# The second SwiGLU product as seven block products in three slabs of K

## The chip, the cores and the metric

The kernel runs on one core of a Trainium2 chip. The metric is the device time of one execution in microseconds (us): 2076.77 us is the median of three runs of the kernel before, which lie between 2076.21 and 2076.93 us. The engines are called PE (matrix products), DVE, ACT and POOL (elementwise work), and SP (which issues the transfers).

## The reference

One layer of a hybrid encoder on 1024 tokens of width 1024, in float32: a normalisation, two mixers in parallel with a residual, then a normalisation, a SwiGLU and a residual, and a last normalisation. The change touches only the SwiGLU and what follows it:

```
def swiglu(xn, w_ffn_in, w_ffn_out):
    gate, up = _split(xn @ w_ffn_in, (D_FF, D_FF))
    return (jax.nn.silu(gate) * up) @ w_ffn_out

h = h + swiglu(rms_norm(h, norm2_g[l]), w_ffn_in[l], w_ffn_out[l])
return rms_norm(h, norm_f)
```

D_FF is 2816, which is 22 tiles of 128. The first product is 1024 tokens by 1024 by 5632, the second 1024 tokens by 2816 by 1024.

## The kernel before

Every large product is done on operands that are split in two: `split` (L79 to L81) casts a float32 source to its high part on ACT and subtracts that from the source on DVE, which gives the low part. A product of two split operands takes three matmuls: high by high, high by low and low by high. The DVE half of a split reads two tensors in SBUF.

The first SwiGLU product goes through 22 units of 128 gate columns and 128 up columns. A unit's weight is four blocks, and so are the tokens, and the four products of a unit come from seven block products instead of eight. POOL makes four sums of weight blocks for each unit (`unit_sums`, L798 to L801), `weight` splits a block or a sum, `product` (L810) issues the matmuls, and `after` adds the banks up. The list `seq` gives the order of the seven products over the units; weights are prepared four products ahead. Each unit's result `act` is written to `act_dram`.

The second product is a plain one. It goes through six pieces of K of 2, 4, 4, 4, 4 and 4 tiles. For each piece and each of the eight groups of 128 tokens, `mm_tok` (L143) runs three matmuls for each tile of K and each half of the columns, and DVE adds the bank to `hres` (L1063; ACT copies it for the first piece, L1061). Its operands are reloaded from `act_dram` and from `w_ffn_out` through `w_raw` (`load_next`, L92) and split by `split_next` once for each group of tokens. The residual `hl` is added to `hres` by POOL (L1055) in the piece that begins at tile 6. In the last piece each group of tokens ends with its own normalisation and two transfers to the output (L1078, L1080); the last group does its second half of columns in two cuts, which go to banks of their own:

```
cuts = (0, 512, 768, 1024) if last and c == NC - 1 else (0, 512, 1024)
...
    po = bank("mm" if c % 2 else "aux")[:, :b - a]
```

All engines run their instructions in the order in which the built program has them. A scheduler puts the instructions of each engine in order when the program is built, so the order is not quite that of the source. Tiles of one tag share a number of buffers (`slot0` and `slot1` have eight each of 8 KB for a partition), and an instruction that writes a new tile waits for the last reader of the buffer that it takes.

Of the kernel before, what the change touches and what calls it, by code (L numbers as in the profile page):

```python
# [32 lines left out]
def hybrid_block_kernel(  # L33
# [426 lines left out]
    with phase("ssd") as pp:  # L460
# [533 lines left out]
    for nk in (2, 4, 4, 4, 4, 4):
        wf = [[], []]
        pieces.append((f0, nk, wf))
        for n in range(2):
            for q in range(nk // 2):
                add_act(f0 + n * (nk // 2) + q)
                add_wf(n, q, f0, wf)  # L1000
        f0 += nk
# [37 lines left out]
    with phase("ffn_out", "right") as pp:  # L1039
        g_bc = pp.tile([P, D], F32, name="g_bc7")  # L1040
        nc.sync.dma_start(out=g_bc, in_=norm_f.unsqueeze(0).broadcast_to([P, D]))

        for f0, nk, wf in pieces:
            last = f0 + nk == NFT
            for c in range(NC):
                if plan or loaded:
                    split_next()
                cuts = (0, 512, 768, 1024) if last and c == NC - 1 else (0, 512, 1024)
                if last:
                    o = pp.tile([P, D], F32, name="o7", tag="o7", bufs=2)  # L1050
                    ss = pp.tile([P, 4], F32, name="ss7", tag="ss7", bufs=3)
                if f0 == 6:
                    hl = pp.tile([P, D], F32, name="hl", tag="hl", bufs=2)
                    nc.sync.dma_start(out=hl, in_=h_dram[c * P:(c + 1) * P, :])
                    nc.gpsimd.tensor_tensor(out=hres[c], in0=hres[c], in1=hl, op=ALU.add)  # L1055
                for i, (a, b) in enumerate(zip(cuts, cuts[1:])):
                    ns, ws = slice(a, b), slice(a % 512, a % 512 + b - a)
                    po = bank("mm" if c % 2 else "aux")[:, :b - a]
                    mm_tok(po, lambda p, k: acts[f0 + k][:, p, c * P:(c + 1) * P], lambda p, k: wf[a // 512][p][:, k, ws], nk)
                    if not f0:  # L1060
                        nc.scalar.copy(out=hres[c][:, ns], in_=po)  # L1061
                        continue
                    nc.vector.tensor_tensor(out=hres[c][:, ns], in0=po, in1=hres[c][:, ns], op=ALU.add)  # L1063
                    if last:
                        nc.scalar.activation(out=o[:, ns], in_=hres[c][:, ns], func=AF.Square, accum_out=ss[:, i:i + 1])
                        if i == 0 and c == NC - 1:
                            nc.gpsimd.tensor_tensor(out=hres[c][:, ns], in0=hres[c][:, ns], in1=g_bc[:, ns], op=ALU.mult)
                if last:
                    nc.vector.tensor_tensor(out=ss[:, 0:1], in0=ss[:, 0:1], in1=ss[:, 1:2], op=ALU.add)
                    if c == NC - 1:  # L1070
                        nc.vector.tensor_tensor(out=ss[:, 0:1], in0=ss[:, 0:1], in1=ss[:, 2:3], op=ALU.add)
                    r = rsqrt_act(pp, ss[:, 0:1], 1.0 / D)
                    for n in range(2):
                        ns = half(n)
                        if n == 0 and c == NC - 1:
                            nc.scalar.activation(out=o[:, ns], in_=hres[c][:, ns], func=AF.Copy, scale=r[:, 0:1])
                        else:
                            nc.vector.scalar_tensor_tensor(out=o[:, ns], in0=hres[c][:, ns], scalar=r[:, 0:1],  # L1078
                                                           in1=g_bc[:, ns], op0=ALU.mult, op1=ALU.mult)
                        nc.sync.dma_start(out=out[c * P:(c + 1) * P, ns], in_=o[:, ns])  # L1080


# [30 lines left out]
```

## Time and profile before

| what | value |
|---|---|
| median of three runs | 2076.77 us |
| profiled execution | 2076.53 us |
| its span, first to last instruction | 2074.8 us |
| granted TensorE clock, mean | 0.993 |
| PE, DVE, ACT, POOL busy | 97%, 59%, 40%, 25% |
| second product in the trace | about 1818.8 to 2066.9 us |

The span is the time between the first and the last instruction of the profiled execution; 1.7 us of its time lie around the span. A PE that is shown busy is pipelined: the rate is read from the distance between groups of matmuls. In a timeline each row has the start, the time taken, the engine, the line, and what it writes and reads; a row can stand for several instructions (x24).

### The profile page before, as it was taken

What the parts mean: (1) busy time and instruction counts of PE and PEld (TensorE: products, weight loads), DVE (VectorE), ACT (ScalarE), POOL (GpSimd) and SP (SyncE); (2) the same over time, 40 slices, a digit from 0 to 9 for tenths busy, and PEclk for the clock granted to TensorE, in tenths of its full rate; (3) what the DMA queues carried; (4) which work ended last, traced back from release to release, by engine and by line L of the source; (5) the groups of instructions that cost most, each with busy time, mean ns of one, the idle gap of its engine ahead of it and who ended that gap; (6) DMA issues with size and microseconds to landing.
All of it is one profiled execution on the core that took longest, in us unless ns stands there. A gap on an engine that the chain in (4) does not pass through costs nothing.

```text
span 2074.8 us, 23723 instructions
## 1 busy us (share of the span) xinstructions
PE 2014.5 (97%) x9212; PEld 1652.6 (80%) x9212; DVE 1215.4 (59%) x1906; ACT 837.7 (40%) x1172; POOL 520.6 (25%) x364
## 2 busy tenths in 40 slices
PE   5999999999999999899999999998999999999998
PEld 4778888878788788688888888886888888888887
DVE  7677676887877877624432123567555555546445
ACT  5877653554544544531131113344323233342112
POOL 3101004525526436300101100036433433303000
PEclk9999999999999999999999999999999999999999
DMA  4221241231322322323232112521232232256212
GB/s 134 62 68 58 61 127 51 88 100 57 92 82 67 110 73 62 101 86 93 63 115 61 51 41 82 191 93 62 72 102 72 71 102 81 76 187 194 82 61 81
DMA packets 178804, 182.27 MB, mean 88 GB/s; under 512 B 9404, under 2 KB 145028, under 8 KB 178692
## 3 DMA queue, kind: packets, MB, share of 16 engines
q1 hardware_dynamic: 178692, 180.76, 28.0%
q8 instruction: 72, 1.18, 0.2%
q14 instruction: 40, 0.33, 0.1%
HBM read 148.10 MB, written 32.64 MB: 87 GB/s over the span
## 4 chain that ended last, share of the span: by engine, by line
PE 78%; DVE 11%; DMA 3%; POOL 2%; issue 2%; ACT 2%; SPq 0%; POOLq 0%; DVEq 0%; ACTq 0%
PE mm L132 35%; PE mm L810 20%; PE mm L143 13%; PE aux L143 6%; DMA ed<-acs_dram 2%; DVE rs_t L155 1%; DVE ed L541 1%; DMA w_raw<-in_w_in_dram 1%; PE aux L421 1%; PE aux L587 1%; DVE rs_r L156 1%; DVE xd L612 1%; DVE wz L81 1%; DVE rs_t L154 1%; PE turn L512 1%
## 5 line engine op out<-in xcount | busy, mean ns | idle before, releaser
L810 PE MATMUL mm<-slot,wc 128*128 128x512 f32 x1848 | 426.9, 392 | 6.3 <-DVE slot L914 5.1
L810 PEld LDWEIGHTS mm<-slot,wc 128*128 128x128 f32 x1848 | 346.9, 188 | 84.7 <-DVE slot L914 6.7
L132 PE MATMUL mm<-xn_hi,w_hi 128*128 128x512 f32 x896 | 354.1, 395 | 1.6 <-DVE xs_a L312 1.1
L132 PE MATMUL mm<-xn_hi,w_lo 128*128 128x512 f32 x896 | 353.3, 395 | 0.0
L132 PE MATMUL mm<-xn_lo,w_hi 128*128 128x512 f32 x896 | 352.2, 393 | 1.1 <-DVE xn_lo L202 1.1
L143 PE MATMUL mm<-slot,slot 128*128 128x512 f32 (+1 forms) x924 | 213.6, 387 | 0.0
L132 PEld LDWEIGHTS mm<-xn_lo,w_hi 128*128 128x128 f32 x896 | 169.2, 189 | 38.7 <-DVE xn_lo L202 1.4
L132 PEld LDWEIGHTS mm<-xn_hi,w_hi 128*128 128x128 f32 x896 | 169.2, 189 | 38.3 <-DVE xs_a L312 1.9
L143 PEld LDWEIGHTS mm<-slot,slot 128*128 128x128 f32 x924 | 171.5, 188 | 34.8
L132 PEld LDWEIGHTS mm<-xn_hi,w_lo 128*128 128x128 f32 x896 | 169.1, 189 | 37.1
L81 DVE TENSOR_TENSOR w_lo<-w_raw,w_hi 128x1024 fp32r<-128x1024 f32 x80 | 108.1, 1351 | 138.4 <-ACT w_hi L80 138.3
L143 PE MATMUL mm<-wz,xn_hi 128*128 128x512 f32 x512 | 164.0, 398 | 0.0
L80 ACT CAST w_hi<-w_raw 128x1024 fp32r<-128x1024 f32 x80 | 83.5, 1043 | 172.9 <-PE mm L132 152.1
L143 PE MATMUL aux<-slot,slot 128*128 128x512 f32 x528 | 124.4, 389 | 0.0
L143 PEld LDWEIGHTS aux<-slot,slot 128*128 128x128 f32 x528 | 99.1, 188 | 20.6
L143 PEld LDWEIGHTS mm<-wz,xn_hi 128*128 128x128 f32 x512 | 96.0, 190 | 18.9
L143 PE MATMUL mm<-wz,xn_lo 128*128 128x512 f32 x256 | 101.8, 398 | 0.0
L848 POOL TENSOR_TENSOR u_u<-u_u,e 128x512 f32<-128x512 f32 x22 | 28.8, 1310 | 248.2 <-DVE u_u L842 238.4
L81 DVE TENSOR_TENSOR wc<-s,wc 128x512 fp32r<-128x512 f32 x88 | 76.4, 908 | 23.0 <-ACT wc L80 23.0
L132 PE MATMUL mm<-v_even,w_hi 128*128 128x512 f32 x256 | 84.7, 405 | 2.2 <-ACT v_even L201 2.2
L132 PE MATMUL mm<-v_odd,w_hi 128*128 128x512 f32 x256 | 81.9, 398 | 0.0
L80 ACT CAST slot<-w_raw 128x1024 fp32r<-128x1024 f32 x34 | 35.5, 1051 | 110.2 <-PE mm L143 50.0
(273 smaller groups left out, 3298.0 us busy)
## 6 DMA issues: line engine op xcount, KB each, us to landing
w_raw<-in_w_in_dram SPq DMA_DIRECT2D x72, 512.0 KB, 3.9
ed<-acs_dram SPq DMA_DIRECT2D x32, 512.0 KB, 3.6
w_raw<-in_w_branch_dram SPq DMA_DIRECT2D x24, 512.0 KB, 3.5
w_raw<-in_w_ffn_in_dram SPq DMA_DIRECT2D x22, 512.0 KB, 4.1
raw_pair<-in_w_ffn_in_dram SPq DMA_DIRECT2D x22, 512.0 KB, 4.3
act_dram<-act SPq DMA_DIRECT2D x22, 512.0 KB, 2.6
act_raw<-act_dram SPq DMA_DIRECT2D x22, 512.0 KB, 3.5
w_raw<-in_w_ffn_out_dram SPq DMA_DIRECT2D x22, 512.0 KB, 4.7
```

The source lines that it names most:

```text
L80: nc.scalar.copy(out=hi, in_=src)
L81: nc.vector.tensor_tensor(out=lo, in0=src, in1=f32(hi), op=ALU.subtract)
L132: nc.tensor.matmul(ps[:m, :], ww[:, k, :], xx(p, k, h), start=(k == 0 and i == 0), stop=(k == nk - 1 and i == 2))
L143: nc.tensor.matmul(ps, xx(p, k), ww(q, k), start=(k == 0 and i == 0), stop=(k == nk - 1 and i == 2))
L154: nc.vector.tensor_tensor(out=t, in0=r, in1=r, op=ALU.mult)
L155: nc.vector.scalar_tensor_tensor(out=t, in0=t, scalar=-0.5, in1=v, op0=ALU.mult, op1=ALU.mult)
L156: nc.vector.scalar_tensor_tensor(out=r, in0=t, scalar=1.5, in1=r, op0=ALU.add, op1=ALU.mult)
L421: nc.tensor.matmul(pg, w[:, j, :], uu[:, hs], start=(q == 0), stop=(q == 2))
L512: nc.tensor.transpose(out=pt[:, i * P:(i + 1) * P], in_=raw[:, o:o + P], identity=ident)
L541: nc.vector.tensor_tensor(out=ed, in0=ed, in1=bcast(acs_t[:, c, hs], P), op=ALU.subtract)
L810: nc.tensor.matmul(ps, w[:, p, k, :], x[q][:, k, :], start=(start and k == 0 and i == 0), stop=(k == 3 and i == 2), skip_group_check=True)
L848: nc.gpsimd.tensor_tensor(out=d["u3"], in0=d["u3"], in1=d["e5"], op=ALU.add)
```

## The change

The second product is written as seven block products instead of eight. Tokens are cut in two halves, columns in two halves, and K in three slabs of 6, 8 and 8 tiles, each cut in two halves of 3, 4 and 4 tiles. In each slab seven products run in the order 1, 2, 6, 7, 5, 4, 3; each has 3 or 4 steps (one for each tile of a half of K), and a step is 12 matmuls of 512 columns, three for each of four groups of tokens. Four loads (roles 1 to 4) bring a quarter of the tokens' operand and a quarter of the weight each, for all steps of a slab; the raw tiles and the split ones share the buffers of `slot0` and `slot1`. For each step's tile of K, eight sums or differences of 128x512 are made of the raw tiles, seven of them on POOL (`slab_sums`, `slab_sums_late`) and one on DVE (L1027). The four banks of a product are added to `hres` or to a sum `vsum` when the product ends.

The two last units of the first product now run side by side in `seq`, and the loads and the first splits of slab 0 are issued during them. The final normalisation is done for tokens 512 to 1023 after product 4 of the last slab and for the others after product 3. The last group of tokens still has its second half in two cuts, both now in one bank.

```diff
+    SLABS = ((0, 3), (6, 4), (14, 4))
...
+    def slab_load(s, role):
+        f0, kk = SLABS[s]
+        i = 1 if role in (1, 3) else 0
+        ti, ka = {1: (0, 0), 2: (0, 1), 3: (1, 0), 4: (1, 1)}[role]
+        kb, dj = {1: (0, 0), 2: (1, 0), 3: (0, 1), 4: (1, 1)}[role]
+        for k0 in range(0, kk, 2):
+            n = min(2, kk - k0)
+            t = pair_tile(i, f"p{role}")
+            fa, fb = f0 + ka * kk + k0, f0 + kb * kk + k0
+            nc.sync.dma_start(out=t[:, :n, 0, :], in_=act_dram[fa * P:(fa + n) * P, half(ti)].rearrange("(k p) m -> p k m", p=P))
+            nc.sync.dma_start(out=t[:, :n, 1, :], in_=w_cols(w_ffn_out, dj * 512, 512, fb * P, n))
...
+    def slab_sums(s, k):
+        p1, p2, p3, p4 = (rawp[s, i, k] for i in range(1, 5))
+        x = xs12[s, k]
+        nc.gpsimd.tensor_tensor(out=x[:, 0], in0=p3[:, 0], in1=p4[:, 0], op=ALU.add)
+        nc.gpsimd.tensor_tensor(out=x[:, 1], in0=p3[:, 1], in1=p1[:, 1], op=ALU.subtract)
+        nc.gpsimd.tensor_tensor(out=p3[:, 0], in0=p1[:, 0], in1=p3[:, 0], op=ALU.subtract)
+        nc.gpsimd.tensor_tensor(out=p1[:, 0], in0=x[:, 0], in1=p1[:, 0], op=ALU.subtract)
+        nc.vector.tensor_tensor(out=p1[:, 1], in0=p4[:, 1], in1=x[:, 1], op=ALU.subtract)
+
+    def slab_sums_late(s, k):
+        p1, p2, p3, p4 = (rawp[s, i, k] for i in range(1, 5))
+        nc.gpsimd.tensor_tensor(out=p3[:, 1], in0=p4[:, 1], in1=p3[:, 1], op=ALU.subtract)
+        nc.gpsimd.tensor_tensor(out=p2[:, 0], in0=p2[:, 0], in1=p1[:, 0], op=ALU.subtract)
+        nc.gpsimd.tensor_tensor(out=p2[:, 1], in0=p2[:, 1], in1=p1[:, 1], op=ALU.subtract)
...
+    y, z = NFT - 2, NFT - 1
+    seq += [(y, 2), (z, 1), (y, 6), (z, 2), (z, 6), (y, 5), (z, 5), (y, 7), (z, 7), (y, 3), (z, 3), (y, 4), (z, 4)]
...
+    EVAC = {1: "11", 2: "11", 6: "v", 7: "22", 5: "22", 4: "21", 3: "12"}
+    ORDER = (1, 2, 6, 7, 5, 4, 3)
...
+    def slab_prepare(i):
...
+        if (s, r, k) not in steps_hl:
+            slab_step(s, r, k)
+        if r == 1 and k == 0:
+            slab_sums_first(s)
+        if r == 2:
+            slab_sums(s, k)
+        if r == 6:
+            slab_sums_late(s, k)
+        if s < 2 and last_k:
+            if r == 6:
+                slab_load(s + 1, 1)
+            elif r == 7:
+                slab_load(s + 1, 3)
+            elif r == 3:
+                slab_load(s + 1, 2)
+                slab_load(s + 1, 4)
...
+    def last_product(ps, kk):
+        for c in range(4):
+            cuts = (slice(0, 512),) if c < 3 else (slice(0, 256), slice(256, 512))
+            for i, cols in enumerate(cuts):
+                for k in range(kk):
+                    step_mm(ps[c], steps_hl[2, 3, k], c, False, k == kk - 1, cols)
+                evac_block(2, 3, c, ps[c], cols)
...
+    SLEAD = 4
```

Three places show what the built program made of it.

POOL from the end of the first product on, before. The names are the units' sums (`u_u`), then the residual sums into `hr`:

```order
L848 TENSOR_TENSOR u_u_13084<-u_u_13084,e_13108 128x512
L848 TENSOR_TENSOR u_u_13214<-u_u_13214,e_13236 128x512
L1055 TENSOR_TENSOR hr_13322<-hr_13322,hl 128x1024
L1055 TENSOR_TENSOR hr_13323<-hr_13323,hl 128x1024
L1055 TENSOR_TENSOR hr_13324<-hr_13324,hl 128x1024
```

The same place now, slab 0. `p_13108` is role 1, `p_13148` role 2, `p_13252` role 3, `p_13172` role 4, each with steps 0 and 1; the names in 13111, 13151, 13255 and 13175 hold step 2 of the same roles. The waits are shown:

```order
L1023 TENSOR_TENSOR x_sums<-p_13252,p_13172 128x512 [waits DMAHW7_49,DMAHW5_49,PE_49]
L1024 TENSOR_TENSOR x_sums<-p_13252,p_13108 128x512 [waits DMAHW4_49,DMAHW0_49]
...
L1024 TENSOR_TENSOR x_sums<-p_13255,p_13111 128x512 [waits DMAHW6_49,DMAHW2_49]
L1025 TENSOR_TENSOR p_13252<-p_13108,p_13252 128x512 [waits Pool_49]
L1031 TENSOR_TENSOR p_13252<-p_13172,p_13252 128x512 [waits DMAHW6_49,Pool_49]
L1033 TENSOR_TENSOR p_13148<-p_13148,p_13108 128x512 [waits DVE_49,Activation_49]
...
L1033 TENSOR_TENSOR p_13151<-p_13151,p_13111 128x512 [waits DMAHW4_49,DVE_49,Activation_49]
L1026 TENSOR_TENSOR p_13108<-x_sums,p_13108 128x512 [waits Pool_49] x2
L1026 TENSOR_TENSOR p_13111<-x_sums,p_13111 128x512 [waits Pool_49]
```

POOL had the eight residual sums there and nothing else. It now has 21 sums, and L1026, whose result product 6 multiplies, stands as the 16th to 18th of them, behind six of L1023 and L1024 and nine of L1025, L1031 and L1033. The first of the 21 waits for a count of PE, which PE reaches as it comes to the slab's first matmul; in slab 1 the count is reached 24 matmuls ahead of the slab, in slab 2 again at its first matmul.

POOL in slab 1, now; `p_13455` and `p_13683` are roles 1 and 2 of steps 2 and 3:

```order
L1032 TENSOR_TENSOR p_13680<-p_13680,p_13452 128x512
L1026 TENSOR_TENSOR p_13455<-x_sums,p_13455 128x512
L1163 TENSOR_TENSOR hr_13331<-hr_13331,hl 128x1024
L1163 TENSOR_TENSOR hr_13332<-hr_13332,hl 128x1024
L1026 TENSOR_TENSOR p_13455<-x_sums,p_13455 128x512
```

The second L1026 here is the one that step 3 of product 6 multiplies. From the slab's first L1023 to it there are 30 instructions, four of them the wide residual sums of L1163; two of those stand right before it. In slab 2 the same count is 29, all of 128x512, with four of L1153 among them.

PE at the program's end, before, where the last group of tokens does its second half in two cuts (the buffers' numbers are kept out; each cut starts a bank of its own):

```order
L143 MATMUL mm<-slot_14352,slot_14518 128x512
L143 MATMUL mm<-slot_14484,slot_14319 128x256
L143 MATMUL mm<-slot_14485,slot_14319 128x256
...
L143 MATMUL mm<-slot_14485,slot_14518 128x256
L143 MATMUL mm<-slot_14484,slot_14518 128x256
```

and now:

```order
L1124 MATMUL aux<-hl_step 128x512 x9
L1124 MATMUL turn<-hl_step 128x512 x3
L1124 MATMUL mm<-hl_step 128x512 x48
L1124 MATMUL aux<-hl_step 128x512 x36
L1124 MATMUL turn<-hl_step 128x256 x24
```

The 24 narrow matmuls of the two cuts now go into one bank of the tag `turn`, and DVE reads the first cut's half of that bank while PE is to write the second.

## Rows read from the trace of the kernel before

**Rows 1.** The page: busy time of the engines, and the chain that ended last.

```profile
PE 2014.5 (97%) x9212; PEld 1652.6 (80%) x9212; DVE 1215.4 (59%) x1906; ACT 837.7 (40%) x1172; POOL 520.6 (25%) x364
...
PE 78%; DVE 11%; DMA 3%; POOL 2%; issue 2%; ACT 2%; SPq 0%; POOLq 0%; DVEq 0%; ACTq 0%
```

**Rows 2.** Windows of the second product: busy of each engine, clock, DMA share, GB/s.

```profile
1818.75:1900.00 81.25, 81.25 (x360) 67.24 (x359) 43.38 (x43) 30.13 (x39) 22.27 (x9) 1.00 0.61 195
1900.00:2000.00 100.00, 100.00 (x443) 82.84 (x442) 49.31 (x59) 21.78 (x21) 0.00 (x0) 1.00 0.33 105
```

**Rows 3.** Groups by line, 1818 to 2075 us: count, busy, mean ns, idle before.

```profile
L143 PE MATMUL aux<-slot,slot 128*128 128x512 f32 x528 | 124.4, 389 | 0.0
L143 PE MATMUL mm<-slot,slot 128*128 128x512 f32 x516 | 121.5, 389 | 0.0
...
L80 ACT CAST slot<-w_raw 128x1024 fp32r<-128x1024 f32 x21 | 22.1, 1052 | 88.4 <-PE mm L143 50.0 <-DMA w_raw<-in_w_ffn_out_dram 38.3
...
L143 PE MATMUL mm<-slot,slot 128*128 128x256 f32 x24 | 3.0, 283 | 0.0
```

**Rows 4.** The chain that ended last, from 2030 us: start, us, what.

```profile
2050.41 5.44 PE mm L143 x24
2055.85 5.44 PE aux L143 x24
...
2065.03 2.50 DVE o L1078 x2
2067.54 0.35 DVE hr L1063
...
2070.37 0.72 ACT o L1076
```

**Rows 5.** Timeline of POOL and DVE in one unit of the first product.

```profile
1689.42 1.32 POOL L798 TENSOR_TENSOR s<-w_raw 128x512 f32<-128x512 f32 x1
1690.08 0.69 DVE L844 TENSOR_TENSOR u_u<-mm,u_u 128x512 f32<-128x512 f32 x1 [2.06 <-PE mm L810]
1690.68 1.32 POOL L800 TENSOR_TENSOR s<-w_raw 128x512 f32<-128x512 f32 x1
...
1691.52 1.03 DVE L851 TENSOR_TENSOR act<-u_u 128x512 f32<-128x512 f32 x1 [0.76 <-ACT u_u L845]
1691.95 1.77 POOL L799 TENSOR_TENSOR s<-s,w_raw 128x512 f32<-128x512 f32 x1
```

**Rows 6.** Timeline of POOL and DVE in the second product.

```profile
1890.83 1.23 DVE L81 TENSOR_TENSOR slot<-w_raw,slot 128x1024 fp32r<-128x1024 f32 x1 [0.17 <-ACT slot L80]
1891.08 3.24 POOL L1055 TENSOR_TENSOR hr<-hr,hl 128x1024 f32<-128x1024 f32 x1 [2.15 <-DMA hl<-h_dram]
1891.97 3.42 DVE L81 TENSOR_TENSOR slot<-act_raw,slot 128x1024 fp32r<-128x1024 f32 x1
...
1896.08 2.40 POOL L1055 TENSOR_TENSOR hr<-hr,hl 128x1024 f32<-128x1024 f32 x1 [1.76 <-DVE hr L1063]
```

**Rows 7.** Windows around an idle stretch of PE in an earlier stage.

```profile
565.80:568.50 2.70, 0.39 (x2) 0.00 (x0) 2.63 (x7) 1.63 (x3) 0.43 (x1) 1.00 0.12 26
...
569.40:572.80 3.40, 3.22 (x8) 2.43 (x8) 3.40 (x6) 0.36 (x1) 1.56 (x1) 0.50 0.55 154
```

**Rows 8.** Timeline of PE in that stretch.

```profile
565.80 0.39 PE L132 MATMUL mm<-xn_lo,w_hi 128*128 128x512 f32 x1
568.72 0.41 PE L552 MATMUL turn<-ident,xs_a 128*128 128x128 f32 x2 [2.53 <-DVE xd L568]
...
570.83 0.63 PE L132 MATMUL mm<-xn_lo,w_hi 128*128 128x512 f32 x1
571.26 0.63 PE L132 MATMUL mm<-xn_hi,w_lo 128*128 128x512 f32 x1
```

**Rows 9.** Issues of transfers: count, KB each, median us to landing.

```profile
act_raw<-act_dram SPq DMA_DIRECT2D x22, 512.0 KB, 3.5
w_raw<-in_w_ffn_out_dram SPq DMA_DIRECT2D x22, 512.0 KB, 4.7
```

More of the change, by code (lines that the diff above doesn't have):

```diff
@@ L994, in hybrid_block_kernel, with pair_tile @@
[L994 to L1001, printed above, removed]
+    SLABS = ((0, 3), (6, 4), (14, 4))
+    rawp, xs12, steps_hl = {}, {}, {}
+    ROLE = {1: (0, 0, 0, 0), 2: (0, 1, 1, 0), 3: (1, 0, 0, 1), 4: (1, 1, 1, 1)}
+    def pair_tile(i, name):
+        t = r8[i].tile([P, 2, 2, 512], F32, name=name, tag=f"slot{i}", bufs=8)
+        return t
@@ new lines, in slab_step @@
+    def slab_step(s, r, k):
+        i = 0 if len(steps_hl) < 3 and s == 0 or (k % 3) else 1
+        t = r8[i].tile([P, 2, 2, 512], F32R, name="hl_step", tag=f"slot{i}", bufs=8)
+        if r in (3, 4):
+            p2, p4 = rawp[s, 2, k], rawp[s, 4, k]
+            for j, src in enumerate((p2[:, 0], p4[:, 1]) if r == 3 else (p4[:, 0], p2[:, 1])):
+                split(t[:, 0, j], t[:, 1, j], src)
+        else:
+            split(t[:, 0], t[:, 1], {1: rawp.get((s, 1, k)), 2: rawp.get((s, 2, k)), 5: xs12.get((s, k)),
+                                     6: rawp.get((s, 1, k)), 7: rawp.get((s, 3, k))}[r])
+        steps_hl[s, r, k] = t
@@ new lines, in slab_sums_first @@
+    def slab_sums_first(s):
+        for k in range(SLABS[s][1]):
+            if k % 2 == 0:
+                x = pair_tile(1, "x_sums")
+            xs12[s, k] = x[:, k % 2]
+    def slab_sums(s, k):
[6 more added lines that the diff above has]
+        nc.vector.tensor_tensor(out=p1[:, 1], in0=p4[:, 1], in1=x[:, 1], op=ALU.subtract)
@@ L1038, in hybrid_block_kernel @@
     hres = [h_pool.tile([P, D], F32, name=f"hr{c}") for c in range(NC)]
[L1039 to L1080, printed above, removed]
@@ new lines, in hybrid_block_kernel, with block_of @@
+    vsum = [h_pool.tile([P, 512], F32, name=f"vs{c}") for c in range(4)]
+    g_bc = h_pool.tile([P, D], F32, name="g_bc7")
+    nc.sync.dma_start(out=g_bc, in_=norm_f.unsqueeze(0).broadcast_to([P, D]))
+    ssq = h_pool.tile([P, 2, NC], F32, name="ssq")
+    sst = h_pool.tile([P, NC], F32, name="sst")
+    ss_end = h_pool.tile([P, 1], F32, name="ss_end")
+    def block_of(r, c):
+        return {"11": hres[c][:, half(0)], "12": hres[c][:, half(1)], "21": hres[4 + c][:, half(0)],
+                "22": hres[4 + c][:, half(1)], "v": vsum[c]}[r]
@@ new lines, in banks_of, with step_mm, evac_block @@
+    def banks_of(i):
+        return [bank(t) for t in (("aux", "aux", "aux", "turn") if i % 2 == 0 else ("mm",) * 4)]
+    def step_mm(ps, t, c, first, last, cols=slice(0, 512)):
+        for i, (p, q) in enumerate(((0, 0), (0, 1), (1, 0))):
+            nc.tensor.matmul(ps[:, cols], t[:, p, 0, c * P:(c + 1) * P], t[:, q, 1, cols], start=(first and i == 0),
+                             stop=(last and i == 2), skip_group_check=True)
+    def evac_block(s, r, c, ps, cols=slice(0, 512)):
+        o = block_of(EVAC[r], c)[:, cols]
+        if s == 0 and r not in (2, 5):
+            nc.scalar.copy(out=o, in_=ps[:, cols])
+        else:
+            nc.vector.tensor_tensor(out=o, in0=ps[:, cols], in1=o, op=ALU.add)
@@ new lines, in hybrid_block_kernel, with square, out_half @@
+    junk = [h_pool.tile([P, 512], F32, name=f"junk{i}") for i in range(2)]
+    def square(n, c):
+        nc.scalar.activation(out=junk[n], in_=hres[c][:, half(n)], func=AF.Square, accum_out=ssq[:, n, c:c + 1])
+    outs = {}
+    def out_half(c, n, r, gained):
+        if c not in outs:
+            outs[c] = stream.tile([P, D], F32, name="o7", tag="w_raw", bufs=2)
+        o, ns = outs[c], half(n)
+        if gained:
+            nc.scalar.activation(out=o[:, ns], in_=hres[c][:, ns], func=AF.Copy, scale=r)
+        else:
+            nc.vector.scalar_tensor_tensor(out=o[:, ns], in0=hres[c][:, ns], scalar=r, in1=g_bc[:, ns],
+                                           op0=ALU.mult, op1=ALU.mult)
+        nc.sync.dma_start(out=out[c * P:(c + 1) * P, ns], in_=o[:, ns])
@@ new lines, in gain, with product_done @@
+    def gain(c, n):
+        nc.gpsimd.tensor_tensor(out=hres[c][:, half(n)], in0=hres[c][:, half(n)], in1=g_bc[:, half(n)], op=ALU.mult)
+    def product_done(s, r, ps):
+        last = s == 2
+        for c in range(4):
+            evac_block(s, r, c, ps[c])
+        if s == 1 and r in (1, 2):
+            for c in range(4 * r - 4, 4 * r):
+                hl = h_pool.tile([P, D], F32, name="hl", tag="hl", bufs=2)
+                nc.sync.dma_start(out=hl, in_=h_dram[c * P:(c + 1) * P, :])
+                nc.gpsimd.tensor_tensor(out=hres[c], in0=hres[c], in1=hl, op=ALU.add)
+        if not last:
+            return
+        if r == 2:
+            for c in range(4):
+                square(0, c)
+        elif r == 6:
+            for b in ("21", "12"):
+                for c in range(4):
+                    o = block_of(b, c)
+                    nc.gpsimd.tensor_tensor(out=o, in0=o, in1=vsum[c], op=ALU.add)
+            for c in range(4):
+                gain(c, 0)
+        elif r == 5:
+            for c in range(4):
+                o = block_of("22", c)
+                nc.gpsimd.tensor_tensor(out=o, in0=o, in1=vsum[c], op=ALU.add)
+                square(1, 4 + c)
+                gain(4 + c, 1)
+        elif r == 4:
+            for c in range(4, 8):
+                square(0, c)
+            nc.vector.tensor_tensor(out=sst[:, 4:8], in0=ssq[:, 0, 4:8], in1=ssq[:, 1, 4:8], op=ALU.add)
+            rr = rsqrt_act(h_pool, sst[:, 4:8], 1.0 / D, 4)
+            for c in range(4, 8):
+                r = rr[:, c - 4:c - 3]
+                out_half(c, 0, r, False)
+                out_half(c, 1, r, True)
@@ new lines, in hybrid_block_kernel @@
+    SLEAD = 4
+    for i in range(SLEAD):
+        slab_prepare(i)
+    chain, n = {}, 0
+    for i, (s, r, k) in enumerate(todo):
+        kk = SLABS[s][1]
+        slab_prepare(i + SLEAD)
+        if k == 0:
+            if r in (1, 2, 7, 5):
+                chain[r] = banks_of(n)
+            n += 1
+        ps = chain[{6: 1, 4: 7, 3: 5}.get(r, r)]
+        if s == 2 and r == 3:
+            if k == kk - 1:
+                last_product(ps, kk)
+            continue
+        for c in range(4):
+            step_mm(ps[c], steps_hl[s, r, k], c, k == 0 and r in (1, 2, 7, 5), k == kk - 1)
+        if k == kk - 1:
+            product_done(s, r, ps)
```

52 lines of the change are left out of this document (30 added, 22 removed).

## The prediction

> **What bounds the kernel now.** I read the page first. PE is busy for 97% of the span and holds 78% of the chain that ended last; POOL is busy for 25% [rows 1]. The change lies in the last eighth of the program, so the windows of that stage come next: between 1819 and 2000 us PE is busy without a gap at the full clock, DVE for about half of the time, and POOL does nothing at all after 1900 us [rows 2]. The groups of that stretch show no idle time before any matmul [rows 3]. So the second product is bound by PE: fewer matmuls are worth their whole time, as long as their operands are there. The chain gives the pace: 24 matmuls in 5.44 us [rows 4], which is 0.227 us for one of 512 columns. Behind the last matmul some 8 us of evacuation, normalisation and transfer follow.
>
> The profiled execution took 2076.53 us, 0.24 us under the median of the runs; sums are made against 2076.5.
>
> **What is removed.** Before there are 528 + 516 matmuls of 512 columns and 24 of 256 [rows 3], as much as 1056 wide ones. Now there are 7 products x 11 steps x 12 = 924, the narrow ones again counted by halves. That takes away 132 x 0.227 = 29.9 us of PE.
>
> **What is added: the sums.** Each step's tile of K needs seven sums on POOL and one on DVE: 77 on POOL in all, against none but the eight residual sums before. What one costs is read from the first product, where POOL makes the same kind of sum: two that follow each other start 1.27 us apart (1689.42, 1690.68, 1691.95), and a wide residual sum takes 2.40 us [rows 5, 6].
>
> Now look at which rows are longer. At 1691.52 DVE begins a product of two SBUF tensors while L800 runs on POOL; it takes 1.03 us and ends 0.60 us after POOL's end, and the L799 behind it takes 1.77 us instead of 1.32. L844, which reads a bank of PSUM and one SBUF tensor, lies beside POOL and costs neither anything [rows 5]. In the second product it is plainer: the split at 1890.83 ends at 1892.06; L1055, asked for at 1891.08, takes 3.24 us and not 2.40; the next split takes 3.42 us and not 1.23, and ends 1.07 us after L1055 [rows 6]. So a POOL sum and a DVE instruction with two SBUF inputs go one after the other, and each split (1.1 us net) or narrow DVE sum (0.6 us net) in a stretch of sums makes that stretch longer by itself.
>
> [...]
>
> **Where the sums stand on the path.** POOL's first sum of a slab waits for PE to come to that slab (slabs 0 and 2) or to 24 matmuls before it (slab 1), because its output takes a buffer that PE still reads. So the sums can't be made ahead; product 6, which multiplies what L1026 writes, is a fixed number of matmuls behind. For each slab I take the step that ends last. Behind L1026 comes a cast of 1.05 us [rows 3].
>
> - Slab 0, step 0 of product 6. POOL does 16 sums: 16 x 1.27 = 20.3, with the cast 21.4 us. PE needs 2 x 3 x 12 = 72 matmuls, 16.3 us. PE waits 5.1 us if nothing is in POOL's way. In the way are DVE's three splits of product 2 and four narrow instructions (three L1027, one L850): 3 x 1.1 + 4 x 0.6 = 5.7. Together 10.8 us.
> - Slab 1, step 3 of product 6. 30 instructions, 26 narrow and 4 of the wide residual sums: 33.0 + 9.6 = 42.6; 24 matmuls ahead of the slab take off 5.4, the cast adds 1.05: 38.3 us. PE needs 132 matmuls, 29.9 us: 8.4 us of waiting. DVE has nine splits and four L1027 in that stretch, 12.3 us. Together 20.7 us. (Steps 0 to 2 wait too, within this sum.)
> - Slab 2, step 3. 29 x 1.27 = 36.8, with the cast 37.9, against 29.9: 8.0 us. DVE has eight splits and four L1027, 11.2 us. Together 19.2 us.
>
> So the three slabs cost between 21.5 us (sums alone) and 50.7 us (all the DVE work between). I take 50.7, because every DVE row that met a POOL row in the trace was held or held it.
>
> [...]
>
> **Smaller terms.** The low half of the step that waited comes one split later: the cast lets four matmuls run (0.9 us), while the split takes 1.1 us and may stand behind one more sum, so 0.2 to 1.5 us, say 0.9, three times: 2.7 us.
>
> [...]
>
> The end: the two narrow cuts of the last group now share a bank, so the second waits for DVE to empty the first. Its own evacuation takes 0.35 us, so with the way there and back 0.6 us at the least; in front of it on DVE may stand final scalings such as the two that took 2.50 us [rows 4], so 3.1 at the most. Final scalings of the other half of the tokens do stand there; I take 2.5. What follows the last matmul is the same chain as before, nothing more, within 1 us.
>
> Costed at nothing: the two last units side by side, whose weights POOL and DVE prepare under the same matmuls (if a bank came late, one evacuation of 0.7 us each). The loads: roles 2 and 4 of the next slab are eight transfers, 4.2 MB, issued five steps (13.6 us) ahead; 195 GB/s at a share of 0.61 is some 320 GB/s, thus 13 us, and one alone lands in 3.5 to 4.7 us [rows 2, 9]. The cover is product 3 of the slab before; if it is too short, POOL starts later by up to 3 us in slabs 1 and 2. Casts on ACT (1.05 us for a step of 2.7 us) have room, and evacuations read PSUM and don't meet POOL.
>
> Sum: -29.9 + 50.7 + 2.7 + 4.8 + 2.5 = +30.8. Predicted: 2107 us.
>
> **The rivals.**
>
> A. The splits don't hold POOL up, or fall where POOL is idle. Then -29.9 + 21.5 + 0.6 (low halves) + 4.8 + 0.6 = -2.4: 2074 us, no change that can be told, or a little faster. For it: DVE is busy for about half of the stage only [rows 2], so that its splits could fall where POOL pauses. Against: POOL has no pause before the gates, and the held instructions of rows 5 and 6.
>
> B. Operands are there in time in every slab, and PE alone decides: -29.9 + 2.5 = 2049 us, faster. For it: POOL has nothing to do after 1900 us [rows 2], and 77 sums are only 98 us of a stage of 210. Against: they are needed in a third of each slab, and the first can't start before the slab. It decides from the point where L1026 of step 0 comes within 16.3 us of the slab's start; 16 sums need 20.3.
>
> C. DVE falls behind as well. A split behind a sum takes 1.1 + 1.27 = 2.4 us, nearly all of a step of 2.7, and DVE has four evacuations of a product (2.8 us) and four L1027 (7.5 us with their waits) on top: 4 x 2.4 + 2.8 + 7.5 = 20 us in a product of 10.9. If that shows up behind product 6 rather than inside its wait, up to 5 us a slab come on top: 2122 us.
>
> **How the numbers follow.** The forecast has 0.73 (on its own 2095 to 2117: 12 us, two fifths of the DVE work in the way, less; or both loads 3 us late, the end and the low halves at their worst, about 9 us more), C 0.15, A 0.07, B 0.05. The range 2088 to 2124 holds the forecast and C and leaves out A and B. A measurement of this kernel tells 0.2%, about 4 us, from no change. Faster by more: B and 0.01 of A, 0.06. Within: 0.05 of A. Slower: the rest, 0.89.
>
> **What would show it.** The timeline of PE should have a gap of about 10 us before the first matmul of product 6 in slab 0, and gaps of some 20 us in all inside product 6 of slabs 1 and 2, each ended by ACT's cast of what L1026 wrote; POOL should run without a pause from the slab's start to that L1026, with sums of 1.3, 1.8 and 2.3 us; the granted clock should dip behind each gap; the matmuls should number 132 fewer in wide ones. Wrong would be: sums that all take 1.3 us (A), no gap at product 6 (B), or gaps ended by DVE behind product 6 (C).

## The result, and the profile after

The changed kernel takes 2109.4 us (median of four executions, 2106.6 to 2116.1) against 2076.85 us in the same series: a ratio of 1.0162, 95% interval 1.0137 to 1.0187, some 33 us slower. A second series gave 2109.1 us and 1.0150 (1.0133 to 1.0166). The profile after is of the slowest execution, 2116.1 us; the one of the second series ("second profile" from here on), of 2108.8 us, is nearer to the median, and sizes are read from it where the two differ.

The page after, answering to [rows 1], then windows of slab 0 and of the places where PE stands, answering to [rows 2], with the same columns:

```profile
PE 2000.7 (95%) x9080; PEld 1635.8 (77%) x9080; DVE 1291.7 (61%) x1931; ACT 877.7 (42%) x1235; POOL 675.3 (32%) x460
```

```profile
1827.75:1843.84 16.09, 16.09 (x72) 13.32 (x71) 14.97 (x11) 5.42 (x7) 16.07 (x10) 1.00 0.66 223
1843.84:1853.50 9.66, 0.39 (x3) 0.01 (x1) 1.21 (x3) 1.04 (x1) 9.66 (x8) 0.66 0.00 0
...
1918.50:1964.00 45.50, 18.07 (x52) 12.28 (x51) 32.59 (x17) 7.97 (x8) 35.63 (x19) 0.65 0.34 115
...
2029.70:2054.40 24.70, 11.45 (x39) 8.01 (x37) 13.81 (x10) 10.96 (x17) 24.70 (x16) 0.81 0.00 1
```

In the first 16 us PE, DVE and POOL are all full; then PE stands for 9.3 us while POOL alone is full. The other two windows are the same place in slabs 1 and 2. The groups of PE, answering to [rows 3], show the removed work and a new column of waiting:

```profile
L1124 PE MATMUL mm<-hl_step 128*128 128x512 f32 x444 | 109.6, 405 | 26.5 <-DVE hl_step L81 16.2 <-ACT hl_step L80 10.3
L1124 PE MATMUL aux<-hl_step 128*128 128x512 f32 x360 | 95.3, 410 | 23.6 <-ACT hl_step L80 23.6
L1124 PE MATMUL turn<-hl_step 128*128 128x512 f32 x108 | 32.5, 398 | 0.0
L1124 PE MATMUL turn<-hl_step 128*128 128x256 f32 x24 | 3.3, 287 | 2.0 <-DVE hr L1132 2.0
```

444 + 360 + 108 + 24/2 = 924 wide matmuls, 132 fewer, as counted. The idle time before them, 52 us, was 0.0 in [rows 3].

Slab 0 in the timeline of PE, then of POOL, then of DVE:

```profile
1839.76 4.47 PE L1124 MATMUL mm<-hl_step 128*128 128x512 f32 x19
1853.50 1.65 PE L1124 MATMUL aux<-hl_step 128*128 128x512 f32 x3 [9.27 <-ACT hl_step L80]
1854.94 0.63 PE L1124 MATMUL turn<-hl_step 128*128 128x512 f32 x1
```

```profile
1827.77 1.30 POOL L1023 TENSOR_TENSOR x_sums<-p,p 128x512 f32<-128x512 f32 x1 [6.24 <-PE mm L810]
1829.02 1.75 POOL L1024 TENSOR_TENSOR x_sums<-p,p 128x512 f32<-128x512 f32 x1
1830.73 2.26 POOL L1023 TENSOR_TENSOR x_sums<-p,p 128x512 f32<-128x512 f32 x1
...
1849.89 1.26 POOL L1033 TENSOR_TENSOR p<-p,p 128x512 f32<-128x512 f32 x1
1851.11 4.73 POOL L1026 TENSOR_TENSOR p<-x_sums,p 128x512 f32<-128x512 f32 x3
```

```profile
1829.54 4.54 DVE L81 TENSOR_TENSOR hl_step<-p,hl_step 128x1024 fp32r<-128x1024 f32 x2
1834.00 1.78 DVE L1027 TENSOR_TENSOR p<-p,x_sums 128x512 f32<-128x512 f32 x1
...
1842.30 2.73 DVE L1132 TENSOR_TENSOR hr<-mm,hr 128x512 f32<-128x512 f32 x4 [0.89 <-PE mm L1124]
```

This is the picture of [rows 5, 6] in earnest. POOL starts as PE reaches the slab and does not pause before L1026 is done. Beside splits and L1027 its sums take 1.75 and 2.26 us; alone they take 1.26, and beside L1132, which reads PSUM, 1.27 to 1.29. L1026 comes 23.3 us after the first sum, ACT's cast follows, and PE goes on, at a granted clock of 0.50 from 1846.9 to 1857.1 us (the row of one matmul shows 0.63 us, where one at 1.00 shows 0.39).

### The profile page after: what moved, and what is told of

Read it like the earlier page. It is cut to its first block, busy times and chain, and to the rows that moved or that the text cites. A ratio compares the mean times of both kernels' runs of the same rounds, so it can differ in the third digit from the quotient of the medians.

```text
span 2114.0 us, 23658 instructions
## 1 busy us (share of the span) xinstructions
PE 2000.7 (95%) x9080; PEld 1635.8 (77%) x9080; DVE 1291.7 (61%) x1931; ACT 877.7 (42%) x1235; POOL 675.3 (32%) x460
## 4 chain that ended last, share of the span: by engine, by line
PE 69%; DVE 13%; POOL 7%; issue 5%; DMA 4%; ACT 3%; SPq 0%; POOLq 0%; DVEq 0%; ACTq 0%
PE mm L132 34%; PE mm L810 19%; PE mm L143 8%; PE mm L1124 2%; DVE rs_t L155 1%; DMA ed<-acs_dram 1%; PE aux L1124 1%; DVE hl_step L81 1%; DVE ed L541 1%; PE aux L421 1%; DMA w_raw<-in_w_in_dram 1%; DVE xd L612 1%; PE aux L587 1%; DVE rs_r L156 1%; DVE rs_t L154 1%
## 5 line engine op out<-in xcount | busy, mean ns | idle before, releaser
L81 DVE TENSOR_TENSOR hl_step<-p,hl_step 128x1024 fp32r<-128x1024 f32 (+1 forms) x88 | 122.4, 1429 | 41.7 <-ACT hl_step L80 41.5
L1124 PE MATMUL mm<-hl_step 128*128 128x512 f32 x444 | 109.6, 405 | 26.5 <-DVE hl_step L81 16.2
L80 ACT CAST hl_step<-p 128x1024 fp32r<-128x1024 f32 (+1 forms) x88 | 69.5, 838 | 147.0 <-POOL p L1026 61.9
L1124 PEld LDWEIGHTS mm<-hl_step 128*128 128x128 f32 x444 | 86.4, 196 | 47.6 <-DVE hl_step L81 18.6
L1124 PE MATMUL aux<-hl_step 128*128 128x512 f32 x360 | 95.3, 410 | 23.6 <-ACT hl_step L80 23.6
L1124 PEld LDWEIGHTS aux<-hl_step 128*128 128x128 f32 x360 | 71.2, 200 | 41.5 <-ACT hl_step L80 26.0
L143 PE MATMUL mm<-slot,slot 128*128 128x512 f32 x384 | 89.2, 391 | 0.0
```

What stands on the lines that cost most here:

```text
L1124: nc.tensor.matmul(ps[:, cols], t[:, p, 0, c * P:(c + 1) * P], t[:, q, 1, cols], start=(first and i == 0), stop=(last and i == 2), skip_gr ...
```

## The experiments

So that the kernels can be compared, the loss of a slab is the distance from its first matmul to that of the next slab, less the number of matmuls times the 0.2267 us of [rows 4] (5.44 / 24); it holds idle time and slow matmuls together. With the low halves on ACT two matmuls of slab 0 ran 8 us ahead, among those of the first product; its slab 0 is counted from the third. The end is the stall before the last narrow cut. In us, from one profile each; in brackets the part of a slab's loss that lies ahead of the step of product 6 that the prediction costed (step 0 in slab 0, step 3 in the others). The kernels ran in different series, so each ratio is to the kernel before in its own series:

| kernel | median us | ratio to before, interval | slab 0 | slab 1 | slab 2 | end |
|---|---|---|---|---|---|---|
| changed, second profile | 2109.1 | 1.0150 [1.0133, 1.0166] | 11.8 (9.4) | 29.5 (16.8) | 18.2 (16.2) | 2.8 |
| low halves on ACT | 2085.9 | 1.0052 [1.0032, 1.0073] | 9.9 (7.0) | 14.7 (13.0) | 12.6 (10.8) | 1.7 |
| sums in source order | 2095.6 | 1.0091 [1.0076, 1.0106] | 9.4 | 18.3 | 16.4 | 3.3 |
| sums on DVE | 2076.3 | 1.0001 [0.9991, 1.0010] | 6.2 | 13.8 | 6.8 | 3.3 |
| all on DVE | 2064.4 | 0.9940 [0.9926, 0.9955] | 2.3 | 5.4 | 7.9 | 0 |
| gain on DVE too | 2063.1 | 0.9931 [0.9916, 0.9946] | 2.4 | 3.8 | 6.8 | 0 |
| adds late | 2103.2 | 1.0124 [1.0109, 1.0140] | 13.1 | 21.4 | 20.4 | 2.5 |
| one cut | 2108.9 | 1.0159 [1.0138, 1.0179] | 11.8 | 29.4 | 18.2 | 0 |
| no residual sums | 2091.6 | 1.0075 [1.0058, 1.0092] | 11.8 (9.4) | 11.7 (9.5) | 18.3 (16.2) | 2.5 |

**Low halves on ACT.** The suspected disturbance is taken away, and DVE's load falls with it.

```diff
+    def split_act(hi, lo, src):
+        nc.scalar.copy(out=hi, in_=src)
+        nc.scalar.copy(out=lo, in_=src)
...
-            split(t[:, 0], t[:, 1], {1: rawp.get((s, 1, k)), ...
+            split_act(t[:, 0], t[:, 1], {1: rawp.get((s, 1, k)), ...
```

> In the slabs' steps the low half of each split is a second copy on ACT (1.05 us for 1024 elements) and no longer DVE's subtraction of two SBUF tensors; the subtraction is left out, so the low halves hold the high part again. Matmuls, sums and POOL's order stay. Theory T1 (a DVE instruction with two SBUF inputs and a POOL sum go one after the other, and that DVE work between the sums is what makes product 6 late by more than the sums alone): POOL's sums take 1.27 to 1.32 us throughout, the gaps before and inside product 6 fall from some 52 us to the sums' own 21.5 us by the prediction's terms, 25 with what two casts for a step add to ACT, and the time is about 2080 to 2090 us. Rival R (the gaps come only from where L1026 stands in POOL's order and from the loads, DVE's splits don't matter): gaps as before, 2103 to 2112 us. If ACT with two copies for a step (2.1 us of 2.7) becomes the bound, the gaps are ended by ACT's copies of other tiles than L1026's, and the time lies over 2095.

Measured: 2085.9 us. The same two groups of POOL, first of the changed kernel, then here (lines are four further down, so L1032 is L1036 and L1026 is L1030); the second number is the mean of one in ns:

```profile
L1032 POOL TENSOR_TENSOR p<-p,p 128x512 f32<-128x512 f32 x11 | 20.3, 1857 | 0.0
L1026 POOL TENSOR_TENSOR p<-x_sums,p 128x512 f32<-128x512 f32 x11 | 17.9, 1635 | 0.0
```

```profile
L1030 POOL TENSOR_TENSOR p<-x_sums,p 128x512 f32<-128x512 f32 x11 | 14.4, 1316 | 0.0
L1036 POOL TENSOR_TENSOR p<-p,p 128x512 f32<-128x512 f32 x11 | 13.8, 1276 | 0.0
```

The order of POOL is the old one, and 23 us are gone. Rival R, for which the splits don't matter, is out. What stays is the sums' own length: slab 0 still loses 7.0 us ahead of product 6, which is the prediction's 5.1 for sums alone and four narrow DVE instructions of 0.45 (the four sums beside them take 1.73 or 1.74 us and not 1.29).

**Sums in source order.** The other half of the cause alone: every POOL sum is wrapped so that the scheduler keeps the order of the source.

```diff
-        nc.gpsimd.tensor_tensor(out=x[:, 0], in0=p3[:, 0], in1=p4[:, 0], op=ALU.add)
+        tc.keep_in_program_order(nc.gpsimd.tensor_tensor(out=x[:, 0], in0=p3[:, 0], in1=p4[:, 0], op=ALU.add))
```

> POOL makes the slabs' sums in the order of the source: per tile of K first L1023 to L1026, so that L1026 of the first tile is the 4th sum of a slab and not the 16th, and those of the later tiles the 8th, 12th, 16th at the latest but for the late sums. All else stays. Rival R (only the place of L1026 in POOL's order is wrong): L1026 lands well ahead of product 6, no gap before product 6, and the time is that of the removed matmuls, 2050 to 2058 us. Theory T1 (POOL's sums and DVE's two-input instructions share one way to SBUF, so that what they need together counts): a tile of K needs 7 sums x 1.27 + 7 splits x 1.1 + one narrow DVE sum 0.6 = 17.2 us of the 19.0 us that its 84 matmuls take; with the residual sums (8 x 2.4 us in slab 1) there is no room in slab 1. The gap before product 6 goes in slab 0, but part of the waiting comes back behind product 6, ended by DVE's low halves (L81) or by the late sums: 2085 to 2105 us.

Measured: 2095.6 us. PE in slabs 0 and 2, then DVE and POOL beside the last of these gaps:

```profile
1860.24 3.98 PE L1124 MATMUL mm<-hl_step 128*128 128x512 f32 x10 [6.03 <-ACT hl_step L80]
```

```profile
2057.94 2.38 PE L1124 MATMUL mm<-hl_step 128*128 128x512 f32 x4 [9.24 <-DVE hr L1132]
```

```profile
2040.26 16.93 DVE L81 TENSOR_TENSOR hl_step<-p,hl_step 128x512 fp32r<-128x512 f32 x10
```

```profile
2044.86 13.46 POOL L1173 TENSOR_TENSOR hr<-hr,vs 128x512 f32<-128x512 f32 x8
```

L1026 now comes in time: no loss ahead of product 6 in slabs 0 and 2. But the wait comes back one product later in slab 0 (6.03 us; ACT's casts wait for L1031 and then L1033, late sums), and in slab 2 ten narrow splits take 16.9 us, 1.69 each, beside POOL's multiplications by the gain (L1153) and its eight sums with `vsum`; the evacuation that PE waits for stands behind them. Order alone gives back 13.5 us of the 62, and the time lies in T1's range and not in rival R's.

**Sums on DVE.** The seven `nc.gpsimd` sums of a tile of K become `nc.vector`.

> All eight sums of a tile of K are made by DVE (0.6 us net for 128x512), none by POOL, which keeps the residual sums L1163 and the sums with vsum alone. Theory T1: a tile of K now needs 8 x 0.6 + 7 x 1.1 = 12.5 us of what DVE and POOL share, against 17.2 of 19.0 before; with the evacuations (0.7 us each) DVE is busy for about 17 of 19 us, so that it just keeps up: the gaps before product 6 shrink to some 10 to 20 us in all, 2070 to 2085 us. Rival D (DVE is the bound then, as its splits and evacuations queue behind eight more sums for a tile): gaps all over the slabs, each ended by DVE, over 2109 us. Rival R (only the place in POOL's order): no gap, 2050 to 2058 us.

Measured: 2076.3 us, no difference from before. What POOL keeps still disturbs: DVE and POOL in slab 1.

```profile
1911.23 2.87 DVE L1033 TENSOR_TENSOR p<-p,p 128x512 f32<-128x512 f32 x1
1914.03 2.82 DVE L1026 TENSOR_TENSOR p<-x_sums,p 128x512 f32<-128x512 f32 x1
```

```profile
1911.08 2.47 POOL L1163 TENSOR_TENSOR hr<-hr,hl 128x1024 f32<-128x1024 f32 x1 [0.86 <-ACT hl_step L80]
1913.87 2.44 POOL L1163 TENSOR_TENSOR hr<-hr,hl 128x1024 f32<-128x1024 f32 x1 [0.31 <-DMA hl<-h_dram]
```

A sum of 0.69 us takes 2.8 beside a residual sum of POOL. Rival D is out by the time: seven more DVE instructions for a tile cost less than seven POOL sums. Its sign is there, though: the 19.8 us for which PE still waits are all ended by DVE. Rival R is out too, since slab 1 still loses 13.8 us.

**All on DVE.** Also `hres + hl`, moved behind products 5 and 4, the sums with `vsum`, source order, and one cut at the end.

```diff
-                nc.gpsimd.tensor_tensor(out=hres[c], in0=hres[c], in1=hl, op=ALU.add)
+                nc.vector.tensor_tensor(out=hres[c], in0=hres[c], in1=hl, op=ALU.add)
...
-                    nc.gpsimd.tensor_tensor(out=o, in0=o, in1=vsum[c], op=ALU.add)
+                    nc.vector.tensor_tensor(out=o, in0=o, in1=vsum[c], op=ALU.add)
```

> All of POOL's work in the second product goes to DVE: the seven sums of a tile of K in the order of the source, the residual sums (put after products 5 and 4 of slab 1) and the sums with vsum; the last group's second half is done in one cut. POOL has nothing left to do there, so nothing holds DVE's two-input instructions up, and L1026 comes early. Theory T1: sums 0.6 us each net, splits 1.1 us, no 2.3 us sums and no 3.4 us splits; DVE is busy for about 17.5 of 19 us per tile of K, with little waiting left at the slabs' beginnings: 2056 to 2070 us, faster than both kernels. Rival D (DVE is the bound): over 2080 us, gaps ended by DVE spread over all products. A rival by which POOL and DVE don't disturb each other would make this slower than the kernel in which POOL makes the sums in the order of the source.

Measured: 2064.4 us, faster than both kernels. The page, the splits, and what PE waits for from 1827 us on (us in total, times, longest), with the same splits in the second profile of the changed kernel behind them:

```profile
PE 1990.8 (96%) x9068; PEld 1629.1 (79%) x9068; DVE 1298.5 (63%) x2026; ACT 878.6 (43%) x1233; POOL 511.3 (25%) x363
```

```profile
L81 DVE TENSOR_TENSOR hl_step<-p,hl_step 128x1024 fp32r<-128x1024 f32 x41 | 49.9, 1225 | 9.6 <-ACT hl_step L80 9.5
L81 DVE TENSOR_TENSOR hl_step<-p,hl_step 128x512 fp32r<-128x512 f32 x44 | 27.9, 682 | 2.3 <-ACT hl_step L80 2.2
```

```profile
PE aux L1124 <- ACT hl_step L80: 5.1, 2, 4.2
PE aux L1124 <- DVE hl_step L81: 2.9, 3, 1.4
PE mm L1124 <- DVE hl_step L81: 2.2, 3, 1.0
```

```profile
L81 DVE TENSOR_TENSOR hl_step<-p,hl_step 128x1024 fp32r<-128x1024 f32 x41 | 75.9, 1874 | 39.7 <-ACT hl_step L80 39.7
L81 DVE TENSOR_TENSOR hl_step<-p,hl_step 128x512 fp32r<-128x512 f32 x44 | 35.0, 844 | 2.2 <-ACT hl_step L80 2.0
```

DVE has 95 instructions more than in the changed kernel and is busy for 7 us more than in its profile above (1298.5 against 1291.7), or 14 more than in the second profile (1284.9). That is far less than the added work, since what DVE did already got shorter: 41 splits that took 1874 ns take 1225 here, 44 narrow ones 682 and not 844, and 11 of L1027 781 and not 1772. PE waits for 10.2 us where it waited for 45.7 in the second profile. Against the kernel before this one, the place of the residual sums, the sums with `vsum`, the order and the cut changed together; no run separates their shares.

**Gain on DVE too.** The last thing of POOL's there.

> As the kernel that has all sums on DVE (2064.35 us), and the eight multiplications by the last gain (L1153) go from POOL to DVE too, four of them to after product 4; POOL then does nothing in the second product. In that kernel's profile the largest gap, 4.4 us before product 6 of slab 2, has POOL's L1153 beside DVE's L1026, L1027 and a split, which took 1.76, 1.75 and 2.29 us and not 0.69, 0.69 and 1.22. Theory T1: these three give back some 3 us, and the time is 2060 to 2063 us. Rival D: DVE has no room for eight more instructions of 0.7 us, and the time is 2064 to 2070 us.

Measured: 2063.1 us. L1026 ahead of product 6 of slab 2, there 1.76 us beside POOL's L1153, is 0.68 here:

```profile
1999.21 1.76 DVE L1026 TENSOR_TENSOR p<-x_sums,p 128x512 f32<-128x512 f32 x1
```

```profile
1996.31 0.68 DVE L1026 TENSOR_TENSOR p<-x_sums,p 128x512 f32<-128x512 f32 x1
```

The gap there falls from 4.2 to 2.5 us. The times of the two kernels are 1.2 us apart, with overlapping intervals: not told apart, so that T1 is borne out by the row but not by the time. It is 46 us faster than the changed kernel in the same series.

**The changed kernel once more.**

> The changed kernel once more, with nothing edited. Its four executions lay between 2106.6 and 2116.1 us, and the profiled one was the 2116.1. In that profile one split of slab 1 (L81 at 1935.61 us) took 12.88 us: it began beside a residual sum of POOL and ended 1.08 us after POOL's first pause, seven POOL instructions later; everywhere else a split waited for one. Theory S: this is a matter of chance in one place, and is what lies between the profiled execution and the others. Then a profile of an execution near 2107 us shows that split at under 4 us and 7 to 10 us less of gaps in slab 1, and one near 2116 shows it again. Rival: it is there in every execution, then a profile near 2107 shows it too, and the difference lies elsewhere.

Measured: 2109.1 us. DVE and POOL at the place in question, first of the 2116.1 us execution, then of the 2108.8 us one:

```profile
1935.61 12.88 DVE L81 TENSOR_TENSOR hl_step<-p,hl_step 128x1024 fp32r<-128x1024 f32 x1 [8.93 <-ACT hl_step L80]
```

```profile
1934.46 4.69 POOL L1163 TENSOR_TENSOR hr<-hr,hl 128x1024 f32<-128x1024 f32 x2
1939.10 1.27 POOL L1026 TENSOR_TENSOR p<-x_sums,p 128x512 f32<-128x512 f32 x1
...
1945.06 2.35 POOL L1163 TENSOR_TENSOR hr<-hr,hl 128x1024 f32<-128x1024 f32 x1
```

```profile
1933.93 5.62 DVE L81 TENSOR_TENSOR hl_step<-p,hl_step 128x1024 fp32r<-128x1024 f32 x2 [8.93 <-ACT hl_step L80]
```

```profile
1932.78 5.68 POOL L1163 TENSOR_TENSOR hr<-hr,hl 128x1024 f32<-128x1024 f32 x2
```

In the first the split ends 1.08 us after POOL's pause at 1947.41, and POOL's instructions keep their undisturbed lengths (1.27 us, and 2.34 to 2.37 for the wide ones); in the second the two engines take turns (5.62 us for two splits, 5.68 for two residual sums). Slab 1 loses 35.3 us in the first and 29.5 in the second, and PE's waits in it are 27.4 and 20.1 us, 7.3 less, as theory S had it. It holds for these two profiles. Why the split lost seven times running is not shown, nor whether a longer execution of the one-cut kernel (2116.2 us, not profiled) had the same cause. An execution of the kernel before, which lacks this stretch, also took 7 us more than the median of this series (2083.8 us), so the length of an execution alone does not tell.

**Adds late.**

```diff
-        if s == 1 and r in (1, 2):
-            for c in range(4 * r - 4, 4 * r):
+        if s == 1 and r in (5, 4):
+            for c in range(4 * (r == 4), 4 + 4 * (r == 4)):
```

> The wide residual sums of slab 1 (L1163, 2.40 us each on POOL) come after products 5 and 4 and no longer after products 1 and 2; nothing else moves. Theory T1 (what POOL does between the slab's start and L1026 decides): four of them, 9.6 us, leave the stretch ahead of L1026 of the last step, and the place where a split waited for seven POOL instructions is gone; they come back beside products 4 and 3, where POOL has time. Gaps in slab 1 fall from 28.9 us to some 15 to 20 us, and the time to 2095 to 2103 us. Rival: the residual sums only stood where POOL would have waited anyway, or are paid again behind product 4, and the time stays at 2105 to 2111 us.

Measured: 2103.2 us, 5.9 less, 0.2 above T1's range and below the rival's. The edit did less than it says: the scheduler still put two of the residual sums ahead of the last L1026, where there had been four, so it is half a test. The loss of slab 1 falls by 8.1 us, but that of slab 2 rises by 2.2, and that of slab 0, which has no residual sums, by 1.3: differences of that size between two profiles have no cause shown.

**One cut.**

> The last group's second half of columns is done in one cut of 512, not in two of 256 that share a bank. The stall of 2.1 us before the second cut goes (the prediction had 2.5), but what follows the last matmul, the evacuation, the square and the sum, is then of 512 columns and not of 256, and all of it behind the last matmul: 0.3 us more for the evacuation, 0.3 for the square, and the first cut's share no longer lies under matmuls. Theory: 0 to 2.5 us faster than the changed kernel. Rival: the stall hid the evacuation that now shows in full, and the time is the same or up to 1 us longer.

Measured: 2108.9 us, the same. The stall is gone (below, the changed kernel's), but from the start of the last matmul to the end it takes 11.8 us and not 9.0. The rival holds: the stall is real, but one cut in place of two does not bring its 2.5 us home.

```profile
2099.97 1.59 PE L1124 MATMUL turn<-hl_step 128*128 128x256 f32 x12
2103.59 1.70 PE L1124 MATMUL turn<-hl_step 128*128 128x256 f32 x12 [2.03 <-DVE hr L1132]
```

**No residual sums.** The block under `if s == 1 and r in (1, 2)` is removed.

> The eight wide residual sums of slab 1 (L1163) and their transfers are left out; all else is the changed kernel. What is open: in a profile of the changed kernel slab 1 is late by 16.8 us where the last step of product 6 begins (the prediction had 20.7) and by 12.7 us more behind it (the prediction had 2.5), where slabs 0 and 2 lose 2.4 and 2.0 there. Theory M: it is the residual sums between the splits that make slab 1 different, four ahead of that step (9.6 us) and four behind it, where splits beside them took 2.76 and 2.95 us. Then slab 1 loses some 7 us ahead and 2.5 behind, 18 to 20 us less in all: 2088 to 2093 us. Rival N: behind product 6 DVE has its own backlog, the splits of five steps and four evacuations, whatever POOL does; then only the 9.6 us ahead of the step are saved: 2098 to 2101 us.

Measured: 2091.6 us. PE in slab 1, in the last step of product 6 and behind it, in the second profile of the changed kernel, then here:

```profile
1947.34 3.76 PE L1124 MATMUL mm<-hl_step 128*128 128x512 f32 x8 [4.33 <-DVE hl_step L81]
1952.23 0.96 PE L1124 MATMUL aux<-hl_step 128*128 128x512 f32 x3 [1.14 <-ACT hl_step L80]
...
1955.21 2.93 PE L1124 MATMUL aux<-hl_step 128*128 128x512 f32 x6 [1.79 <-DVE hl_step L81]
```

```profile
1937.93 2.11 PE L1124 MATMUL mm<-hl_step 128*128 128x512 f32 x8 [1.72 <-DVE hl_step L81]
1939.88 0.84 PE L1124 MATMUL aux<-hl_step 128*128 128x512 f32 x3
```

The low half of the step itself came 4.3 us late in the changed kernel and 1.7 here; product 7 waited for two more operands and waits for none here. Slab 1 loses 9.5 us ahead of the step and 2.2 behind its start: theory M. Without POOL's wide sums between them, DVE works its splits off in time (behind the step's start 1.21 to 1.23 us each, where the changed kernel's took 2.30 and 2.95). The transfers of the residual are gone with the sums; no run separates the two.

## Why the prediction was right, and where its sizes were not

By its own steps, against the second profile, in us:

| step | predicted | measured |
|---|---|---|
| 132 fewer matmuls (by count, at 0.2267 us) | -29.9 | -29.9 |
| ahead of product 6, slab 0 | 10.8 | 9.4 |
| slab 1 | 20.7 | 16.8 |
| slab 2 | 19.2 | 16.2 |
| behind it: low halves 2.7, clock 4.8 | 7.5 | 2.4 + 12.7 + 2.0 = 17.1 |
| end | 2.5 | 2.8 |
| sum | +30.8 | +32.4 |

The sum agrees with the times (2108.8 - 2076.5 = 32.3), and the mechanism is shown: the place of L1026 (by the source order), DVE's two-input instructions that lengthen the stretch (by the low halves on ACT), and the two together, which leave 15.6 us of the 62 when all is on one engine. Two sizes were off, in opposite directions, -8.3 and +9.6 us; that the total is only 1.6 us off is luck.

- Ahead of product 6 the three stretches were costed 8.3 us too long. POOL's own rows say where: from the slab's first sum to the end of the L1026 in question it took 24.6 us in slab 0, 50.8 in slab 1 and 44.8 in slab 2, where the prediction's counts make 26.0, 54.9 and 48.0. "Every DVE row" was the upper bound, and some of them overlap with less than their length: in slab 0 a split's share is 9.4 - 7.0 = 2.4 us for three, not 3.3. In all three slabs the loss ahead of product 6 falls by 11.6 us (42.4 to 30.8) when the splits leave DVE, where the prediction had 22 for twenty splits; a second cast on ACT for each step may hide some of that. Another 10.7 of the 23 us that the low halves on ACT give back lie behind product 6 (17.1 to 6.4).
- Behind it, the step that failed is the low halves and the clock, 7.5 us for 17.1. The prediction let the low half stand behind one more POOL sum, 0.2 to 1.5 us. In slab 1 it stands behind a split of another product and an evacuation, and each of the two splits waits for an instruction of POOL, the second for the first of the four residual sums that come after L1026, which the prediction had at no cost (DVE there, in the second profile; the last row is the low half that PE waits 4.3 us for):

```profile
1941.69 2.31 DVE L81 TENSOR_TENSOR hl_step<-x_sums,hl_step 128x1024 fp32r<-128x1024 f32 x1
1943.92 0.68 DVE L1132 TENSOR_TENSOR hr<-turn,hr 128x512 f32<-128x512 f32 x1
1944.52 2.76 DVE L81 TENSOR_TENSOR hl_step<-p,hl_step 128x1024 fp32r<-128x1024 f32 x1
```

Without residual sums slab 1 loses 2.2 us there and not 12.7. This is rival C's mechanism, DVE late behind product 6; it was given up to 5 us for each slab, and came as about 10 us in slab 1 and nothing in the others.

The clock is a part of both. In the second profile these are two of the six stretches after 1840 us at a granted clock of 0.50, before the program's tail (columns as in [rows 2]):

```profile
1845.10:1855.30 10.20, 3.43 (x8) 2.76 (x9) 3.44 (x2) 3.14 (x4) 10.20 (x8) 0.50 0.00 0
1927.10:1940.70 13.60, 5.86 (x12) 3.64 (x12) 6.77 (x4) 3.89 (x4) 13.60 (x9) 0.50 0.19 60
```

All six hold 8 + 12 + 8 + 14 + 7 + 7 = 56 matmuls, and 56 x (0.43 - 0.227), with the distance of [rows 8], is 11.4 us. No run shows the 4.8 us that the prediction's sum has for the clock, which is three times the 1.6 us that the 8 matmuls of the one stretch at 0.50 in [rows 7, 8] cost: 8 x (0.43 - 0.227). Of the 56, 27 lie ahead of a later wait of the same slab, which they shorten; how much, no run separates.

Rival A is refuted by the low halves on ACT: taking the splits off DVE is worth 23 us. The trace shows a POOL sum and a DVE instruction with two SBUF inputs one after the other (the sum takes 2.26 us beside a split, 1.26 alone); the 12.88 us split, which outlasted seven POOL instructions, is more than one such wait. Rival B needed the sums ahead of time, and the kernel with all on DVE, 2064 us, comes within 15 us of its 2049 without getting there.

## What to carry to other kernels

Two engines whose instructions the trace shows one after the other, as POOL's sums and DVE's splits here (1.26 us alone, 2.26 beside a split), are to be costed as one: add up those instructions, per tile of work, and compare with PE's time for that tile, before an engine with a low busy share is called free. A sum that gates a product is costed from the first instant its buffer is free, in the engine's built order, with everything that stands ahead of it; and what stands behind the gate, between the next operands, is counted as well. Moving elementwise work to the faster of the two engines can shorten the kernel, even when that engine looks busier: here 77 sums moved from POOL (32% busy, 1.26 us for a sum alone) to DVE (61%, 0.69 us) took some 32 us off.

## What had not been expected of the hardware

A waiting DVE instruction didn't always get the next turn here: beside POOL instructions that followed each other without a pause one split waited for seven of them, 12.88 us, in one of two profiles of the same program, at the same place where in the other the engines took turns (5.62 us for two splits). And more work cost DVE little: with 95 instructions more its busy time rose by 7 to 14 us, while without POOL's sums a wide split took 0.65 us less on the mean (1225 against 1874 ns). That kernel is 45 us faster than the changed one, with the new order of the sums a part of it.
